# A step of a hybrid diffusion backbone: the first adaLN weights loaded in six large transfers ahead of an order of their own

## The chip, the cores and the metric

The kernel runs on one core of one Trainium2 chip. The metric is the device time of one execution in microseconds. It is written in a tile language that turns Python calls into instructions for five engines: TensorE (PE, with its weight loads shown as PEld), VectorE (DVE), ScalarE (ACT), GpSimd (POOL) and SyncE (SP), which issues all of the kernel's DMA transfers.

## What is computed

Two layers of a backbone, on 128 context tokens and 256 latent tokens together (384 columns), width 1024, all in float32. Cut to what matters here:

```python
mod = silu(c) @ w_ada[l] + b_ada[l]
shift1, scale1, gate1, shift2, scale2, gate2 = split(mod, 6)
h = rms_norm(x) * (1 + scale1) + shift1
out = mix(h)
x = x + gate1 * out
h = rms_norm(x) * (1 + scale2) + shift2
x = x + gate2 * ((silu(a_) * b_) @ w_ffn_out)
```

`mix` projects `h` with `w_in`, runs three token mixers (a state-space scan called SSD, attention, and an mLSTM), gates and merges them. So the first projection of layer 0 needs `shift1` and `scale1` of layer 0, and these need the product of a small vector with 1024 x 2048 weights (8 MB). These weights are called the first adaLN weights here.

## The kernel before

All weights lie in one array `ws` of pieces of 128 x 1024 floats (512 KB each), in the order in which they are used. `piece` (L639) loads the next piece into one of four buffers `raw` and, for a dense product, splits it on ScalarE into a high part `wh` and on VectorE (or GpSimd) into a rest `wl`, so that three fast products (`HH` with `wh`, `HL` with `wh`, `HH` with `wl`) give a float32 result; `HH` and `HL` are the two parts of the normed input. One dense piece is 8 k-tiles of three matmuls.

`setup` (L780) loads the conditioning vector (`sil`), constants (`cst`), biases (`bada`), and `x` into the slot `PH`. `ada` (L732) is called for four groups u = 0, 2, 1, 3, each with four pieces: 128 small matmuls of 32 columns with the weights `silc`, a transposition by `ident`, and an addition of the bias into `mod`. Groups 0 and 2 give shift and scale for k-tiles 0 to 3, groups 1 and 3 for 4 to 7. Meanwhile `ssq` squares x, `norm_end` (L834) makes the row factors `nacc`, and `modulate` (L858) writes `HH` and `HL`, k-tile by k-tile.

The SSD stage (`ssd`, L1002) goes over 8 pairs of heads in each layer. For a pair, `ex` (two buffers) is loaded from `rowe` by DMA and multiplied on GpSimd with `pb`; `decays` (L973) makes a decay matrix in `PH` from `PL`, which is loaded from `rowr`: VectorE writes it, ScalarE takes its exponential, GpSimd sums two halves (`PH<-PH`), VectorE multiplies it (`PH<-PH,PL`). Then TensorE adds up the pair's output in the bank `l`. Dense pieces of the projections that come later, and the attention's preparation (`E` and `D`: norms and the rotary products with `pT`), stand between the pairs.

The order of the work is not the order of the code. A recorder keeps every operation, and `order` (L376) plays a list schedule with estimated costs: whichever operation is ready and has the smallest key goes next on its engine. The key is the place in the code plus a bias set by `urgency`: FEED for loads and splits, EVAC for what empties a bank, DENSE for dense products. The costs come from `Clock` (TensorE's two rates, and a price for a change of the matmul's tile shape) and `cost`. `emit` (L503) then writes the instructions in that fixed order, at line 509, so each engine works through its own list in order; the profile shows nearly everything under L509, and tiles are told apart by name.

Of the kernel before, what the change touches and what calls it, by code (L numbers as in the profile page):

```python
# [222 lines left out]
class Recorder:  # L223
# [86 lines left out]
    class Clock:  # L310
# [9 lines left out]
        def run(self, now, work):  # L320
# [3 lines left out]
            for cols, rows, fixed, tile in work:  # L324
                if tile != self.tile:
                    now += 0.09
                    self.tile = tile
                    while now >= self.end:
                        self.tick()
                while True:  # L330
                    rate = 2400.0 if self.warm else 1200.0
                    done = min(cols, (self.end - now) * rate)
                    self.count += done * rows
                    now += done / rate
                    cols -= done
                    if cols <= 1e-6:
                        break
                    self.tick()
                if self.warm:
                    now += fixed  # L340
                while now >= self.end:
                    self.tick()
# [3 lines left out]
    def cost(eng, meth, args, kw):  # L346
# [17 lines left out]
        if eng == "sync":  # L364
            big, run = max(int(np.prod(v.shape)) for v in args[:2]), min(_run(v) for v in args[:2])
            rows = big / run
            return 0.36, rows * (0.025 + run * 4 * 0.0000415) / 16, 1.3 + min(rows, 256) * 0.0085

# [159 lines left out]
FEED, EVAC, DENSE = -60000, -30000, 60000  # L528

ND, NM, NL = 3, 4, 1  # L530
NR = 4

AHEAD = 14
# [6 lines left out]
class Net:  # L540
# [98 lines left out]
    def piece(self, key, split=True):  # L639
# [6 lines left out]
        with self.urgency(FEED):  # L646
            for _ in range(cnt):
                raw = self.buf("wp", "raw", [P, 1024], NR)
                self.dma(raw, self.I["ws"][self.ppos])
                self.ppos += 1  # L650
# [81 lines left out]
    def ada(self, l, u):  # L732
        raws = self.piece(("ada", l, u), split=False)
        ps = self.dps()
# [45 lines left out]
    def setup(self):  # L780
# [6 lines left out]
        self.cst = lambda n: cst[:, CST[n][0]:CST[n][0] + CST[n][1]]  # L787
        self.ident = self.cst("ident")
        self.badas = []
        for l in range(LAYERS):  # L790
            b = self.const(f"bada{l}", [P, 48])
            self.dma(b, I["cols"][l, :, COLS["bada"][0]:COLS["bada"][0] + 48])
            self.badas.append(b)
        self.dma(self.x, I["xT"])
        self.ones = self.const("ones", [P, P])
# [606 lines left out]
    def run(self):  # L1402
        self.setup()
        for u in (0, 2, 1, 3):
            self.ada(0, u)
        for j in range(8):
# [80 lines left out]
def layout(a):  # L1487
# [18 lines left out]
    for key, n in st:  # L1506
# [21 lines left out]
        ws[pos:pos + n] = v.reshape(P, n, 1024).transpose(1, 0, 2)  # L1528
        pos += n
    out["ws"] = ws  # L1530
    x = np.concatenate([A["x_prompt"].reshape(P, D), A["x_sample"].reshape(256, D)], axis=0)
# [63 lines left out]
```

## Time and profile before

| | us |
|---|---|
| runs | 1969.58, 1973.36, 1974.23 (median 1973.36) |
| the profiled execution's own time | 1967.48 |
| its span, first to last instruction | 1965.7 |
| TensorE busy in the span | 1904.1 (97%) |
| VectorE busy | 1295.0 (66%) |
| ScalarE busy | 951.7 (48%) |
| GpSimd busy | 371.7 (19%) |
| DMA engines, share of 16 | 53.1% for the kernel's own queue |

The profile is one execution. Busy shares are means over stages that differ: TensorE is busy nearly without a gap in most of the span, and its gaps lie in a few places. For the change the stretches at the start and the views of single engines in time order say more than the page's sums. A row of the timeline gives start, duration, engine, source line, operation, what is written and read, how many in a row, and in brackets how long the engine had been idle and on what it waited.

### The profile page before, as it was taken

To read this page: it belongs to the slowest core of one execution; us is meant where nothing else is said; L and a number is where in the kernel's file an instruction comes from. 1 tells how busy PE (TensorE), PEld (TensorE's weight loads), DVE (VectorE), ACT (ScalarE), POOL (GpSimd) and SP (SyncE) were. 2 spreads that over 40 slices of the span, in tenths; PEclk is the share of its full clock that TensorE was granted. 3 is DMA by queue.
4 is the path that set the end of the run, shared out by engine and by line. 5 is a ranking of instruction groups with operands and counts; after the bars stand their busy time and mean duration, and the time that the engine had idled before them with its cause. 6 is when DMAs were issued, how large, how long until landed. Compare 5 with 4: busy or idle time off the path is not lost. (4 is left out here: it accounts for less than half of the span.)

```text
span 1965.7 us, 30591 instructions
## 1 busy us (share of the span) xinstructions
PE 1904.1 (97%) x11202; PEld 1731.0 (88%) x11202; DVE 1295.0 (66%) x2733; ACT 951.7 (48%) x1910; POOL 371.7 (19%) x355
## 2 busy tenths in 40 slices
PE   5999999999999999999999897999999999999997
PEld 4987898789888999999999775987888999999997
DVE  4956889777745666655358677877767567666622
ACT  3654666665522444443346554666555334444421
POOL 0134433110002210001211244330000023000121
PEclk8999999999999999999999998999999999999998
DMA  8565546434488666566654655464344555444441
GB/s 298 128 173 180 151 142 193 139 107 119 128 305 273 217 193 198 188 194 193 202 184 132 163 160 124 133 184 131 116 113 145 157 169 160 118 127 129 127 124 61
DMA packets 120342, 318.33 MB, mean 162 GB/s; under 512 B 13824, under 2 KB 57216, under 8 KB 119424
## 3 DMA queue, kind: packets, MB, share of 16 engines
q1 hardware_dynamic: 120192, 316.38, 53.1%
q8 instruction: 88, 1.44, 0.3%
q14 instruction: 62, 0.51, 0.1%
HBM read 295.54 MB, written 19.74 MB: 160 GB/s over the span
## 5 line engine op out<-in xcount | busy, mean ns | idle before, releaser
L509 ACT ACTIVATE wh<-raw 128x1024 fp32r<-128x1024 f32 x374 | 396.0, 1059 | 559.9 <-PE d L509 485.1
L509 DVE TENSOR_TENSOR wl<-raw,wh 128x1024 fp32r<-128x1024 f32 x335 | 437.0, 1305 | 226.9 <-ACT wh L509 219.2
L509 PE MATMUL d<-HH,wh 128*128 128x384 f32 x1448 | 495.1, 349 | 1.6 <-ACT E L509 0.7
L509 PE MATMUL d<-HL,wh 128*128 128x384 f32 x1416 | 467.4, 336 | 0.0
L509 PE MATMUL d<-HH,wl 128*128 128x384 f32 x1384 | 465.4, 336 | 0.9 <-DVE wl L509 0.9
L509 PEld LDWEIGHTS d<-HH,wh 128*128 128x128 f32 x1448 | 272.3, 189 | 27.0 <-issue 19.2
L509 PEld LDWEIGHTS d<-HL,wh 128*128 128x128 f32 x1416 | 266.6, 189 | 1.3 <-issue 0.8
L509 PEld LDWEIGHTS d<-HH,wl 128*128 128x128 f32 x1384 | 260.5, 188 | 1.4 <-DVE wl L509 1.4
L509 PE MATMUL d<-A,wh 128*128 128x386 f32 x744 | 254.8, 342 | 0.0
L509 PE MATMUL d<-C,wh 128*128 128x386 f32 x744 | 251.5, 338 | 0.0
L509 PE MATMUL d<-A,wl 128*128 128x386 f32 x744 | 250.1, 336 | 0.0
L509 POOL TENSOR_TENSOR wl<-raw,wh 128x1024 fp32r<-128x1024 f32 x39 | 94.4, 2420 | 473.3 <-ACT sh L509 361.0
L509 PEld LDWEIGHTS d<-A,wh 128*128 128x128 f32 x744 | 139.9, 188 | 13.0 <-issue 10.9
L509 PEld LDWEIGHTS d<-C,wh 128*128 128x128 f32 x744 | 140.6, 189 | 0.4
L509 PEld LDWEIGHTS d<-A,wl 128*128 128x128 f32 x744 | 139.9, 188 | 0.0
L509 POOL TENSOR_TENSOR sc<-sc,sc 128x126 f32<-128x126 f32 x112 | 69.4, 638 | 222.8 <-DVE sc L509 203.6
L509 DVE SCALAR_TENSOR_TENSOR PH<-PL,n,cst 128x128 f32<-128x128 f32 x288 | 98.0, 375 | 16.6 <-DMA PL<-rowr 13.5
L509 DVE TENSOR_TENSOR sc<-d,nacc 128x384 f32<-128x384 f32 x93 | 51.8, 557 | 78.2 <-PE d L509 73.9
L509 PE MATMUL d<-wh,HH 128*128 128x512 f32 x240 | 98.6, 411 | 0.1
L509 PE MATMUL d<-wl,HH 128*128 128x512 f32 x240 | 94.3, 393 | 0.0
L509 PE MATMUL d<-wh,HL 128*128 128x512 f32 x240 | 94.2, 393 | 0.0
L509 PE MATMUL d<-PH,wh 128*128 128x384 f32 x256 | 87.1, 340 | 0.0
(237 smaller groups left out, 3090.6 us busy)
## 6 DMA issues: line engine op xcount, KB each, us to landing
raw<-in_ws SPq DMA_DIRECT2D x470, 512.0 KB, 3.7
PL<-rowr SPq DMA_DIRECT2D x48, 384.0 KB, 5.5
gd<-sc SPq DMA_DIRECT2D x48, 192.0 KB, 2.4
pb<-gd SPq DMA_DIRECT2D x48, 192.0 KB, 2.7
ex<-rowe SPq DMA_DIRECT2D x32, 128.0 KB, 4.0
ex<-rowe SPq DMA_DIRECT2D x16, 256.0 KB, 5.3
PH<-in_xT SPq DMA_DIRECT2D x2, 1536.0 KB, 7.3
yad<-pb SPq DMA_DIRECT2D x16, 192.0 KB, 1.9
```

The lines of the kernel that those rows point to most:

```text
L509: tc.keep_in_program_order(getattr(engines[op.eng], meth)(*[real(a) for a in args], **{k: real(v) for k, v in kw.items()}))
```

## The change

It has four parts.

- The sixteen first adaLN pieces are no longer loaded one by one into `raw`. Six transfers of 2 or 3 pieces each (FIRST_LOADS) go into slots of the later stages that are still unused: A, C, E, F, D and PL. In `ws` these pieces are laid out so that one row of such a transfer is 8 or 12 KB in one piece on both sides, instead of 4 KB.
- Setup, `x` and groups 0 and 2 get the key FIRST, groups 1 and 3 the key SECOND, and the loads of the first three dense pieces the key FIRST as well, so that these stand behind groups 0 and 2 and ahead of groups 1 and 3.
- The load of `x` moves out of `setup` to the place right behind it, ahead of all weights.
- In the planner, a change of tile shape on TensorE costs 0.18 (0.33 after the shape (4, 1), which is 128 rows by 32 columns, as in the adaLN products) instead of 0.09, and a transfer's cost per row and per byte is different. These numbers move no work by themselves; they change which operation the planner takes next, everywhere in the program.

```diff
-                    now += 0.09
+                    now += 0.33 if self.tile == (4, 1) else 0.18
...
-            return 0.36, rows * (0.025 + run * 4 * 0.0000415) / 16, 1.3 + min(rows, 256) * 0.0085
+            return 0.36, rows * (0.036 + run * 4 * 0.0000337) / 16, 1.3 + min(rows, 256) * 0.0085
...
+FIRST, SECOND = -120000, -110000
...
+FIRST_LOADS = ((0, 3, "A"), (3, 3, "C"), (6, 2, "E"), (8, 3, "F"), (11, 3, "D"), (14, 2, "PL"))
+
+AHEAD_OF_SECOND = 3
...
-                self.dma(raw, self.I["ws"][self.ppos])
+                with self.urgency(FIRST if self.ppos < 16 + AHEAD_OF_SECOND else FEED):
+                    self.dma(raw, self.I["ws"][self.ppos])
...
     def ada(self, l, u):
-        raws = self.piece(("ada", l, u), split=False)
+        key, cnt = self.stream[self.spos]
+        assert key == ("ada", l, u), key
+        self.spos += 1
+
+        for pos, n, tag in FIRST_LOADS:
+            if pos in (self.ppos, self.ppos + 3, self.ppos + 6) and self.ppos % 8 == 0:
+                home = self.slot(tag, [P, n, 1024])
+                self.dma(home.rearrange("p n c -> p (n c)"),
+                         self.I["ws"][pos:pos + n].rearrange("n p c -> (n p c)").rearrange("(p m) -> p m", p=P))
+                self.homes += [home[:, i] for i in range(n)]
+        raws = [self.homes.pop(0) for _ in range(cnt)]
+        self.ppos += cnt
...
-        self.dma(self.x, I["xT"])
...
     def run(self):
-        self.setup()
+        with self.urgency(FIRST):
+            self.setup()
+            self.dma(self.x, self.I["xT"])
         for u in (0, 2, 1, 3):
-            self.ada(0, u)
+            with self.urgency(SECOND if u % 2 else FIRST):
+                self.ada(0, u)
...
+    for at, n, _ in FIRST_LOADS:
+        ws[at:at + n] = ws[at:at + n].transpose(1, 0, 2).reshape(n, P, 1024)
```

How it moves instructions is seen in the order in which they stand on the engines. The numbers behind a name are buffers, counted anew in each program, so they differ between the two.

**SP, the start.** Before, SP's first rows are these:

```order
L509 DMA raw_80<-in_ws 128x1024
L509 DMA raw_84<-in_ws 128x1024
L509 DMA raw_86<-in_ws 128x1024
L509 DMA raw_88<-in_ws 128x1024
L509 DMA K_90<-in_ckT 128x128 x2
L509 DMA sil_2_93<-in_cT 128x16
L509 DMA cst_95<-in_cst 128x395
L509 DMA bada_4_97<-in_cols 128x48
L509 DMA bada_5_99<-in_cols 128x48
L509 DMA PH_101<-in_xT 128x3072
L509 DMA cols_103<-in_cols 128x215
```

After three rows with the conditioning vector, the constants and the first bias, SP has now:

```order
L509 DMA bada_5_88<-in_cols 128x48
L509 DMA PH_90<-in_xT 128x3072
L509 DMA A_92<-in_ws 128x3072
L509 DMA C_94<-in_ws 128x3072
L509 DMA E_96<-in_ws 128x2048
L509 DMA raw_98<-in_ws 128x1024
L509 DMA raw_102<-in_ws 128x1024
L509 DMA raw_106<-in_ws 128x1024
L509 DMA F_108<-in_ws 128x3072
L509 DMA D_110<-in_ws 128x3072
L509 DMA PL_112<-in_ws 128x2048
L509 DMA raw_114<-in_ws 128x1024
```

The four adaLN pieces that stood first are gone, x moved ahead of all weights, the three `raw` between E and F are dense pieces, and the loads of `K` and `cols` moved behind everything.

**TensorE, the end of the adaLN products.** Before, the third group (`d_259`), the broadcast of the row factors (`m_310`), the fourth group (`d_341`) and the first dense row:

```order
L509 MATMUL d_259<-raw_230,silc_82 32x128 x8
L509 MATMUL m_310<-sc_298,ones_78 128x384
L509 MATMUL d_259<-raw_245,silc_82 32x128 x8
L509 MATMUL d_338<-cst_95,sc_333 128x128
L509 MATMUL d_341<-raw_272,silc_82 32x128 x8
L509 MATMUL d_341<-raw_292,silc_82 32x128 x8
L509 MATMUL d_341<-raw_312,silc_82 32x128 x8
L509 MATMUL d_341<-raw_326,silc_82 32x128 x8
L509 MATMUL d_404<-cst_95,sc_402 128x128
L509 MATMUL d_422<-HH_329,wh_406 128x384
L509 MATMUL d_422<-HL_336,wh_406 128x384
```

Now, from the second group's transposition (`d_236`) on, with the third group `d_269`, the broadcast `m_302`, the fourth group `d_319` and the first dense piece `d_376`:

```order
L509 MATMUL d_236<-cst_84,sc_231 128x128
L509 MATMUL d_269<-F_108,silc_82 32x128 x24
L509 MATMUL m_302<-sc_280,ones_78 128x384
L509 MATMUL d_269<-D_110,silc_82 32x128 x8
L509 MATMUL d_319<-D_110,silc_82 32x128 x4
L509 MATMUL d_328<-cst_84,sc_317 128x128
L509 MATMUL d_319<-D_110,silc_82 32x128 x12
L509 MATMUL d_319<-PL_112,silc_82 32x128 x16
L509 MATMUL d_376<-HH_321,wh_224 128x384
L509 MATMUL d_376<-HL_334,wh_224 128x384
L509 MATMUL d_376<-HH_321,wl_234 128x384
L509 MATMUL d_388<-cst_84,sc_374 128x128
```

The first dense rows stand right behind the last adaLN product and ahead of its transposition (`d_388`); the broadcast still stands behind most of the third group.

**TensorE and GpSimd, SSD in layer 1.** The third, fourth and fifth pair of heads of layer 1 write the banks `l_11751`, `l_11805`, `l_11877` before. On TensorE, from the last dense row ahead of the third pair to the fourth pair's last:

```order
L509 MATMUL d_11579<-wl_11633,HH_10157 128x512
L509 MATMUL l_11751<-PH_11157,xn_11331 64x128 x2
L509 MATMUL l_11751<-ex_11318,c_1951_11326 64x256 x2
L509 MATMUL l_11751<-PH_11157,xn_11331 64x256 x4
L509 MATMUL m_11775<-cst_95,A_10466 128x128 x3
L509 MATMUL m_11783<-pb_11778,bn_10966 64x128 x2
L509 MATMUL l_11805<-PH_11157,xn_11585 64x128 x2
L509 MATMUL l_11805<-ex_11560,c_1959_11568 64x256 x2
L509 MATMUL l_11805<-PH_11157,xn_11585 64x256 x4
```

Now these three pairs are `l_11661`, `l_11785` and `l_11857`; the third pair and what follows it:

```order
L509 MATMUL l_11661<-PH_11130,xn_11310 64x128 x2
L509 MATMUL l_11661<-ex_11293,c_1941_11300 64x256 x2
L509 MATMUL l_11661<-PH_11130,xn_11310 64x256 x4
L509 MATMUL d_11583<-wh_11579,HH_10137 128x512
L509 MATMUL d_11583<-wh_11579,HL_10146 128x512
L509 MATMUL d_11583<-wl_11591,HH_10137 128x512
L509 MATMUL m_11695<-cst_84,A_10446 128x128 x3
```

Before, no dense row stood between the third and the fourth pair, nor up to the fifth, and 177 between the fifth and the sixth. Now 33 dense matmuls stand between the third and the fourth, none up to the fifth, and 36 between the fifth and the sixth. From the dense rows' total since the transpositions of the row factors, 273 stood ahead of the third pair, now 252, and ahead of the fourth and fifth 273, now 285.

On GpSimd at the same place, before (`ex_11761` is the fifth pair's, `D_11534` the attention's rotary product):

```order
L509 TENSOR_TENSOR D_11534<-D_11534,pT_5745 128x512
L509 TENSOR_TENSOR D_11534<-D_11534,pT_5853 128x8x32 x4
L509 TENSOR_TENSOR PH_11157<-PH_11157 128x384 x2
L509 TENSOR_TENSOR pb_11778<-xn_11771,we_11209 128x256
L509 TENSOR_TENSOR ex_11761<-ex_11761,pb_11033 128x512
L509 TENSOR_TENSOR PH_11157<-PH_11157 128x384 x2
L509 TENSOR_TENSOR pb_11831<-xn_11825,we_11209 128x256
L509 TENSOR_TENSOR ex_11815<-ex_11815,pb_11033 128x512
```

and now (`ex_11672` is the fifth pair's):

```order
L509 TENSOR_TENSOR PH_11130<-PH_11130 128x384 x2
L509 TENSOR_TENSOR pb_11693<-xn_11685,we_11194 128x256
L509 TENSOR_TENSOR PH_11130<-PH_11130 128x384
L509 TENSOR_TENSOR ex_11672<-ex_11672,pb_11011 128x512
L509 TENSOR_TENSOR D_11568<-D_11568,pT_5631 128x512
L509 TENSOR_TENSOR D_11568<-D_11568,pT_5771 128x8x32 x4
L509 TENSOR_TENSOR PH_11130<-PH_11130 128x384 x2
L509 TENSOR_TENSOR pb_11812<-xn_11805,we_11194 128x256
```

Before, the five rotary rows of `D` stood ahead of the third pair's second sum; now they stand behind both sums of the third pair and the fifth pair's `ex`, and ahead of the fourth pair's second sum.

## Rows read from the trace of the kernel before

**Rows 1.** Busy time of each engine in three stretches (count in brackets), clock, DMA, GB/s.

```profile
0.00:50.00 50.00, 29.65 (x314) 22.61 (x315) 21.92 (x70) 16.32 (x37) 2.64 (x12) 0.90 0.84 293
50.00:1100.00 1050.00, 1042.01 (x6094) 937.44 (x6093) 708.09 (x1466) 525.11 (x1036) 199.36 (x199) 1.00 0.57 177
1100.00:1250.00 150.00, 130.05 (x661) 105.55 (x661) 105.04 (x221) 74.37 (x139) 60.09 (x57) 0.92 0.55 148
```

**Rows 2.** Timeline of ScalarE and TensorE, 29 to 46.2 us: start, duration, work.

```profile
29.62 0.49 ACT L509 ACTIVATE nacc<-m 128x384 f32<-128x384 f32 x1 [4.58 <-PE m L509]
...
36.80 1.08 PE L509 MATMUL d<-raw,silc 128*32 128x128 f32 x16 [2.31 <-DMA raw<-in_ws]
...
39.28 0.69 PE L509 MATMUL d<-HH,wh 128*128 128x384 f32 x1 [0.47 <-ACT wh L509]
...
41.19 0.69 PE L509 MATMUL d<-HH,wl 128*128 128x384 f32 x1 [0.90 <-DVE wl L509]
...
45.52 0.49 PE L509 MATMUL d<-HH,wh 128*128 128x384 f32 x1
...
45.84 0.35 PE L509 MATMUL d<-HL,wh 128*128 128x384 f32 x1
...
46.02 0.33 PE L509 MATMUL d<-HH,wl 128*128 128x384 f32 x1
```

**Rows 3.** Stretches of the transfers, columns as in rows 1.

```profile
3.50:13.00 9.50, 2.95 (x56) 2.73 (x60) 0.35 (x2) 0.21 (x1) 0.00 (x0) 1.00 1.02 388
...
14.50:19.50 5.00, 1.84 (x21) 1.28 (x20) 3.73 (x11) 2.93 (x8) 0.00 (x0) 1.00 1.01 404
...
32.00:38.00 6.00, 2.42 (x52) 1.34 (x48) 3.58 (x11) 2.07 (x5) 0.00 (x0) 0.80 0.96 362
...
39.28:45.84 6.56, 5.66 (x17) 5.16 (x18) 6.56 (x13) 4.16 (x8) 0.00 (x0) 0.50 0.67 200
...
671.00:676.00 5.00, 5.00 (x31) 5.00 (x30) 2.52 (x3) 1.36 (x2) 0.00 (x0) 1.00 0.92 362
```

**Rows 4.** Timeline of TensorE in layer 1, 1184 to 1203 us.

```profile
1184.98 0.39 PE L509 MATMUL d<-wh,HL 128*128 128x512 f32 x1
...
1185.20 0.39 PE L509 MATMUL d<-wl,HH 128*128 128x512 f32 x1
...
1192.85 0.48 PE L509 MATMUL l<-PH,xn 128*64 128x128 f32 x1 [6.89 <-DVE PH L509]
...
1202.48 0.47 PE L509 MATMUL l<-PH,xn 128*64 128x128 f32 x1 [4.46 <-DVE PH L509]
```

**Rows 5.** Timeline of GpSimd in layer 1, 1178 to 1200 us.

```profile
1178.70 2.21 POOL L509 TENSOR_TENSOR D<-D,pT 128x512 f32<-128x512 f32 x1 [1.90 <-DVE D L509]
...
1181.54 4.22 POOL L509 TENSOR_TENSOR D<-D,pT 128x256 f32<-128x256 f32 x4 [0.63 <-DVE D L509]
...
1199.12 1.45 POOL L509 TENSOR_TENSOR ex<-ex,pb 128x512 f32<-128x512 f32 x1 [1.80 <-DMA ex<-rowe]
```

**Rows 6.** Chain of waits in time order: start, us, what; 1194 to 1202 us.

```profile
1194.92 4.04 DMA ex<-rowe
...
1200.54 1.04 POOL PH L509
```

**Rows 7.** Timeline of SP, first 8 us: start, duration, line, transfer, count.

```profile
0.73 1.81 SPq L509 DMA_DIRECT2D raw<-in_ws  x4
...
3.85 0.44 SPq L509 DMA_DIRECT2D sil<-in_cT  x1
...
4.34 0.47 SPq L509 DMA_DIRECT2D cst<-in_cst  x1
...
4.85 1.19 SPq L509 DMA_DIRECT2D bada<-in_cols  x2
...
7.26 0.33 SPq L509 DMA_DIRECT2D PH<-in_xT  x1
```

**Rows 8.** Tile raw, first 60 us, its last line.

```profile
DMA to landing us min/median/max: 3.5/4.8/6.7
```

More of the change, by code (lines that the diff above doesn't have):

```diff
@@ L788, in setup @@
         self.ident = self.cst("ident")
+        self.homes = []
         self.badas = []
```

## The prediction, on record before the changed kernel was run

> **What bounds the kernel now.** I read first the busy time of the engines in long stretches [rows 1]. TensorE is busy for 1042.0 of the 1050 us between 50 and 1100: there it is the bound, and no earlier transfer helps. Two stretches differ. In the first 50 us it is busy for 29.65, so 20.35 us are idle, and between 1100 and 1250 us for 130.05 of 150, so 19.95 are idle. The change works on the first by its code and on the second by the planner's new prices.
>
> Then the timeline at the start. TensorE's dense work begins at 39.28 us, but only from 41.19 does it run on: its first row of the low part waited 0.90 for `wl` [rows 2]. Ahead of that it worked on the last adaLN piece at 36.80, for which it had waited 2.31 on the DMA [rows 2]. So transfers set the beginning, and behind them a short chain: product, transposition, split of the first dense piece. The transfers run at 388 to 404 GB/s where the queue is full, at 362 just before the last piece lands [rows 3].
>
> Last, layer 1's SSD stage. TensorE waits 6.89 us before the third pair and 4.46 before the fourth, both for VectorE's `PH` [rows 4]; the chain of waits shows why the fourth takes 9.63 us after the third (1202.48 less 1192.85): a load of `ex` of 4.04 us, GpSimd's multiplication, then GpSimd's sum of `PH`, which stands behind it in GpSimd's list [rows 4 to 6].
>
> **Term 1, the beginning.** SP now starts with `sil`, `cst` and two `bada`: 0.44 + 0.47 + 1.19 = 2.1 us [rows 7], and gaps. So `x` is issued near 3.0, where before the first large load went out at 0.73. A 512 KB load lands 3.5 us after its issue at the shortest [rows 8]; take off SP's 0.33 and 1.3 for 524 KB at 395 GB/s, and 1.9 us are left for its start and its end together. I take 1.0 for each, so the stream runs from 4.0. From there to the last adaLN piece it carries `x`, A, C, F and D of 1536 KB, E and PL of 1024 KB and three dense `raw` of 512 KB: 11264 KB = 11.53 MB. None of these waits for a buffer, where before SP waited for a free `raw` after every four pieces.
>
> The rate is not known for six large loads in a row. Rows: 404 GB/s with 512 KB loads, 388 with x among them, 362 in 32 to 38 us, and 362 around the second load of x, whose rows are 12 KB like the new ones [rows 3]. Nothing there is faster for long rows, so I take 395, between the first two because their queue was full as the new one will be. That is 29.2 us; the last byte moves at 33.2, and with the 1.0 for its end PL has landed at 34.2. The Trainium skill has a limit against this: DMA: Bandwidth & Descriptors, section Where 436 GB/s comes from, puts what HBM gives one core at about 358 GB/s and says that it binds for loads; by it the burst would take 32.2 us. The trace disagrees with its 404 over 5 us, though its 362 would fit.
>
> Then 16 small matmuls at 1.08 us [rows 2] bring 35.3. The first dense rows stand right behind, their weights split long before, so the old 2.5 us from the last product's start to the first dense row and the 0.90 for `wl` fall away; the transposition among them costs about 0.5. Is the normed input ready? The broadcast of the row factors stands behind most of the third group, which needs F: 8.91 MB, landed near 27.6. Its 24 small matmuls (1.6), itself (1.0) and ScalarE's copy of 0.49 end at 30.7, against 30.1 before [rows 2]; then ScalarE must first copy the third group's result, which needs D at 31.5, and the first k-tile is there near 33.5. That is before 35.3, and TensorE's list runs two further dense pieces on the early k-tiles while VectorE writes the later ones. `cols`, now behind PL, lands near 36 and can hold VectorE for under 1 us; `K`, `c` and the rotary table are wanted much later.
>
> The clock: at 39.28 to 45.84 the granted clock is 0.50, 1.2 GHz, and matmuls follow each other every 0.32 us; at 45.84 the next comes after 0.18, at 2.4 GHz [rows 2, 3]. TensorE had waited before. It will have waited now, too, so I let as many run at the low level: 17 of them from 35.8 on, 5.4 us, to 41.2, where before 17 were done at 45.84 [rows 3]. **Gain 4.6.** Ends: at 404 GB/s, where the burst takes 28.5, 5.3; at 362, where it takes 31.9, 1.9; and below nothing a loss of 5.6 at 293, the mean of the first 50 us with all waits for buffers in it [rows 1], which I take for a far end only.
>
> **Term 2, layer 1's SSD stage.** Work there is the same, the order is not. Before TensorE reaches the third pair it has now 21 dense matmuls fewer behind it, at 0.22 [rows 4] 4.6 us: near 1180.9 instead of 1185.5. VectorE's and GpSimd's part of that pair no longer stands behind the attention's products of `D` (2.21 + 4.22 us on GpSimd) [rows 5], which is what made it late, so I let this wait go. What is late next is the fourth pair: its second sum now stands behind the fifth pair's `ex` and behind the products of `D`. From the third pair's start: 2.07 until the load (1194.92 less 1192.85), 4.04 for it, the multiplication with its start 6.27 after and 1.45 long, 6.43 for the products, and 1.9 from the sum to the matmul (1202.48 less 1200.54) [rows 4 to 6]: 16.1, or 17 with an estimated 0.9 for VectorE's sum of the products. So the fourth pair starts near 1198, 4.5 earlier than at 1202.48, and TensorE has done 12 more dense matmuls by then, 2.6 us. The link to the fifth pair stays. Between the fifth and the sixth there are only 36 dense matmuls, 6.5 us at 0.18, against a link of 9.63: 3.1 lost. **Gain 4.5 + 2.6 - 3.1 = 4.0.** Ends: a whole link, 9.6, if the third pair comes earlier still; nothing below, for the third pair may stay late, which is a rival.
>
> **Other edits.** Elsewhere the new prices move some 5% of TensorE's rows. Where it is busy nearly throughout, a swap of ready work costs nothing; I put 0, with 2 either way for layer 0's SSD stage, whose pairs keep at least 39 dense matmuls between them. The new layout in `ws` is made before the run.
>
> **Sum.** 4.6 + 4.0 = 8.6. Against the profiled execution's own 1967.48 that is 1958.9. This execution is 5.9 below the median of the runs, 1973.36; set against that median, **1964.8 us**.
>
> **Rivals.** *Only the beginning gains.* If the waits of layer 1 merely change places, 4.6 is left: 1968.8. For it: two links are unfilled before and after. *The burst runs at 362 GB/s*, as just before the last piece: term 1 is 1.9, the time with term 2 is 1967.5. For it: that is also the rate around the second x load [rows 3]; against: the 404. By the limit of the Trainium skill named above it would be nearly the same. *The dense weights do not help:* they delay the last adaLN piece by 1.57 MB, 4.0 us, and if the row factors come late (F and D later than reckoned), TensorE waits for `HH` instead; term 1 is then 0 and the time 1969.4. *Slower:* the rotary products of `D`, now behind the fifth pair's `ex` on GpSimd, hold the fourth pair. If the third pair comes as late as before, at 1192.85, the fourth comes 17 later, near 1209.9, 7.4 after its old time, and with 3.1 before the sixth pair 10.5 are lost, if VectorE holds the dense pieces' splits back as well; less 4.6, that is 1979.3. It decides from the third pair's start: with these 3.1, later than about 1187 the stage eats the whole of term 1.
>
> **How the numbers follow.** Both terms as reckoned 0.50, its own range 1957 to 1970; only the beginning 0.15; slow burst 0.15; dense weights no help 0.06; slower 0.14. About 0.3%, 5.9 us, is what a measurement can tell from no change. Faster by more: 0.45 of the first, 0.04 + 0.06 + 0.01 of the next three: 0.56. Slower by more: 0.09 of the last, 0.01 + 0.02 from others: 0.12. Between: 0.32. The range 1955 to 1976 leaves out most of the slower case and gains over 18 us, some 0.16.
>
> **What would show it.** Right: PL lands at 33 to 36, dense rows run on from about 36, at 2.4 GHz from about 41 to 42; the third pair without a wait, the fourth some 17 us behind it; under 17 us idle between 1100 and 1250. Wrong: a first dense row that waits for `HH`; transfers well below 388 GB/s from 5 to 33 us; more idle in layer 1; or new gaps between 50 and 1100.

## The result: slower, and not where the change works

The changed kernel took **1986.68 us** (median of 4 runs, 1985.74 to 1986.97), the kernel before 1973.37 (4 runs, 1969.58 to 1974.23): a ratio of 1.007 (95% interval 1.0053 to 1.0088), 13 us slower, where 8.6 us less had been forecast. A second measurement on another chip gave 1.0079 (1.0066 to 1.0092). The profiled execution of the change took 1986.97 us, its span is 1985.2, 19.5 more than before.

TensorE's busy time on the page of the changed kernel:

```profile
span 1985.2 us, 30537 instructions
...
PE 1927.5 (97%) x11202; PEld 1745.8 (88%) x11202; DVE 1292.5 (65%) x2733; ACT 950.8 (48%) x1910; POOL 364.3 (18%) x355
```

Before, the same 11202 matmuls were busy for 1904.1 us. So on the whole TensorE doesn't wait longer; it is busy 23.4 us longer with the same work. Busy times in the stretches of [rows 1], changed kernel (columns: stretch, its length, PE, PEld, DVE, ACT, POOL busy with counts, granted clock, share of the DMA engines, GB/s):

```profile
0.00:50.00 50.00, 29.13 (x347) 24.27 (x348) 23.40 (x72) 18.75 (x40) 2.84 (x12) 0.90 0.76 293
50.00:1100.00 1050.00, 1044.96 (x6010) 934.34 (x6011) 694.88 (x1449) 514.30 (x1023) 191.99 (x195) 1.00 0.58 176
1100.00:1250.00 150.00, 130.74 (x653) 101.73 (x652) 105.68 (x219) 73.89 (x137) 57.85 (x56) 0.91 0.53 146
```

The first 50 us went about as forecast: 347 matmuls instead of 314, so 33 more, which is 5.8 us at 0.176. Then between 50 and 1100 us TensorE is busy 2.95 us longer and does 84 matmuls fewer. There most of the loss arises, in the stretch to which the prediction gave 0: layer 1's SSD stage, whose first matmul is shown below, begins 12.6 us later than before.

What makes TensorE slower can be seen in two pieces of the chain of waits in which nothing but dense matmuls stands (start, us, what, count). The first is 912 matmuls of 384 columns from `HH`, `HL`, `PH` and `PL`; the second 1512, two thirds of 386 columns from `A` and `C`. The kernel before:

```profile
1512.73 158.14 PE d L509 x912
1678.21 264.42 PE d L509 x1512
```

The changed kernel:

```profile
1526.32 160.89 PE d L509 x912
1694.74 267.62 PE d L509 x1512
```

Per matmul that is 173.4 ns before and 176.4 now (158.14 and 160.89 by 912), and 174.9 and 177.0 in the second. The first piece begins 13.6 us later than before, the span ends 19.5 later, and the 5.9 between are these two pieces, 2.75 and 3.20 longer. TensorE waits for nothing there, the clock is granted at 1.00, the weights and operands are the same numbers. Only two things differ: the order of instructions, and the place of the tiles in SBUF (the on-chip memory from which TensorE reads). With `PH`, `A`, `C`, `E`, `F`, `D` and `PL` wanted first, as homes for `x` and the adaLN weights, they are also allocated first. In the built programs `HH` begins at byte 80800 of each partition before and at 154112 now, counted modulo 256 at 160 and at 0. The same for others: `HL` 160 and 0, `D` 160 and 0, `PL` 224 and 0, `F` 64 and 0, `A` 160 and 224, `C` 64 and 32; `PH` 224 in both. All weights (`wh`, `wl`) begin at 160 in both.

The beginning itself, timeline of TensorE in the changed kernel (start, duration, work):

```profile
34.77 1.06 PE L509 MATMUL d<-PL,silc 128*32 128x128 f32 x32
35.76 0.44 PE L509 MATMUL d<-HH,wh 128*128 128x384 f32 x1
36.04 0.34 PE L509 MATMUL d<-HL,wh 128*128 128x384 f32 x1
36.22 0.33 PE L509 MATMUL d<-HH,wl 128*128 128x384 f32 x1
```

The first dense row stands at 35.76 (35.3 had been forecast; 39.28 before [rows 2]) and has not waited; the next come after 0.28 and 0.18, so at 2.4 GHz from the second on, where 17 at 0.32 had been put in.

Layer 0's SSD stage has a wait that was not there before. TensorE and GpSimd in the changed kernel, timeline:

```profile
168.48 0.44 PE L509 MATMUL m<-pb,bn 128*64 128x128 f32 x4 [3.01 <-POOL pb L509]
```

```profile
165.60 1.27 POOL L509 TENSOR_TENSOR ex<-ex,pb 128x512 f32<-128x512 f32 x1 [4.88 <-DMA ex<-rowe]
166.82 1.60 POOL L509 TENSOR_TENSOR pb<-xn,we 128x256 f32<-128x256 f32 x1
```

The product `pb`, for which TensorE waits, stands on GpSimd behind a product of `ex` that waits 4.88 us for a load. And behind TensorE's wait of 3.01 us the granted clock falls to 1.2 GHz, stretches of the changed kernel:

```profile
160.00:169.50 9.50, 6.49 (x40) 5.93 (x39) 8.09 (x21) 5.36 (x12) 3.54 (x3) 1.00 0.54 157
169.50:180.00 10.50, 10.50 (x30) 7.82 (x30) 3.84 (x14) 3.29 (x6) 2.28 (x2) 0.51 0.60 129
180.00:190.00 10.00, 10.00 (x56) 7.36 (x55) 2.87 (x4) 3.36 (x8) 7.44 (x7) 1.00 0.41 116
```

So in this execution a wait of 3.0 us costs another 5: 10.5 us are busy throughout at half the clock, with 30 matmuls where the next 10 us have 56.

Layer 1's SSD stage, timeline of TensorE: first the stage's first matmul in the kernel before,

```profile
1126.81 0.36 PE L509 MATMUL m<-cst,pb 64*128 64x64 f32 x1 [4.92 <-ACT pb L509]
```

then the changed kernel, from the same matmul to the second half of the fourth pair, the place of the waits in [rows 4]:

```profile
1139.37 0.36 PE L509 MATMUL m<-cst,pb 64*128 64x64 f32 x1 [7.67 <-ACT pb L509]
...
1191.73 0.44 PE L509 MATMUL l<-PH,xn 128*64 128x128 f32 x4
...
1202.19 0.43 PE L509 MATMUL l<-PH,xn 128*64 128x128 f32 x2
...
1212.37 0.48 PE L509 MATMUL l<-PH,xn 128*64 128x128 f32 x1 [9.74 <-DVE PH L509]
```

and GpSimd beside it:

```profile
1196.49 1.43 POOL L509 TENSOR_TENSOR ex<-ex,pb 128x512 f32<-128x512 f32 x1 [0.59 <-DMA ex<-rowe]
1198.90 7.32 POOL L509 TENSOR_TENSOR D<-D,pT 128x512 f32<-128x512 f32 x5 [0.98 <-DVE D L509]
1210.30 1.15 POOL L509 TENSOR_TENSOR PH<-PH 128x384 f32<-128x384 f32 x1 [4.08 <-ACT PH L509]
```

The third pair (1191.73) no longer waits, as forecast. The fourth waits 9.74 in its second half, 20.6 us behind the third pair's start. Idle time between 1100 and 1250 is 19.3 us, against 19.95, but this window holds other work now, for the stage begins later.

### The profile page after: what moved, and what is told of

Read it like the earlier page. It is cut to its first block, busy times and chain, and to the rows that moved or that the text cites. A ratio compares the mean times of both kernels' runs of the same rounds, so it can differ in the third digit from the quotient of the medians.

```text
span 1985.2 us, 30537 instructions
## 1 busy us (share of the span) xinstructions
PE 1927.5 (97%) x11202; PEld 1745.8 (88%) x11202; DVE 1292.5 (65%) x2733; ACT 950.8 (48%) x1910; POOL 364.3 (18%) x355
## 5 line engine op out<-in xcount | busy, mean ns | idle before, releaser
L509 ACT ACTIVATE wh<-raw 128x1024 fp32r<-128x1024 f32 x374 | 396.0, 1059 | 580.1 <-PE d L509 506.4
L509 DVE TENSOR_TENSOR wl<-raw,wh 128x1024 fp32r<-128x1024 f32 x335 | 432.1, 1290 | 257.6 <-ACT wh L509 254.0
L509 PE MATMUL d<-HH,wh 128*128 128x384 f32 x1448 | 499.4, 352 | 0.2 <-ACT sc L509 0.2
L509 PE MATMUL d<-HL,wh 128*128 128x384 f32 x1416 | 472.8, 339 | 0.0
L509 PE MATMUL d<-HH,wl 128*128 128x384 f32 x1384 | 469.3, 339 | 0.0
L509 PEld LDWEIGHTS d<-HH,wh 128*128 128x128 f32 x1448 | 272.1, 189 | 24.4 <-issue 20.2
L509 PEld LDWEIGHTS d<-HL,wh 128*128 128x128 f32 x1416 | 266.4, 189 | 2.0 <-issue 0.8
L509 PEld LDWEIGHTS d<-HH,wl 128*128 128x128 f32 x1384 | 260.6, 188 | 0.0
L509 PE MATMUL d<-A,wh 128*128 128x386 f32 x744 | 255.6, 344 | 0.0
L509 PE MATMUL d<-A,wl 128*128 128x386 f32 x744 | 252.5, 339 | 0.0
L509 PE MATMUL d<-C,wh 128*128 128x386 f32 x744 | 251.9, 339 | 0.0
L509 POOL TENSOR_TENSOR wl<-raw,wh 128x1024 fp32r<-128x1024 f32 x39 | 93.5, 2397 | 462.7 <-ACT sh L509 365.2
L509 PEld LDWEIGHTS d<-A,wh 128*128 128x128 f32 x744 | 140.0, 188 | 13.0 <-issue 12.6
L509 PEld LDWEIGHTS d<-C,wh 128*128 128x128 f32 x744 | 140.7, 189 | 0.4
L509 PEld LDWEIGHTS d<-A,wl 128*128 128x128 f32 x744 | 140.3, 189 | 0.0
L509 DVE SCALAR_TENSOR_TENSOR PH<-PL,n,cst 128x128 f32<-128x128 f32 x288 | 99.4, 382 | 20.4 <-DMA PL<-rowr 15.4
L509 DVE TENSOR_TENSOR sc<-d,nacc 128x384 f32<-128x384 f32 x93 | 51.8, 557 | 82.6 <-PE d L509 78.0
L509 POOL TENSOR_TENSOR sc<-sc,sc 128x126 f32<-128x126 f32 x112 | 65.7, 606 | 194.0 <-DVE sc L509 148.8
L509 PE MATMUL d<-wh,HH 128*128 128x512 f32 x240 | 100.8, 420 | 0.0
L509 PE MATMUL d<-wh,HL 128*128 128x512 f32 x240 | 95.7, 399 | 0.0
L509 PE MATMUL d<-wl,HH 128*128 128x512 f32 x240 | 95.4, 398 | 0.0
L509 PE MATMUL d<-PH,wh 128*128 128x384 f32 x256 | 87.4, 341 | 0.0
```

Of the source, the lines that this page charges most:

```text
L509: tc.keep_in_program_order(getattr(engines[op.eng], meth)(*[real(a) for a in args], **{k: real(v) for k, v in kw.items()}))
```

## The experiments

The theory from here on: **address.** The distance of dense matmuls (from one start to the next) depends on where their two operands begin in SBUF, and the new order of allocation moved them to a worse place. The rival: **order.** The distance comes from the new order of instructions, which the planner's prices made, or from `wh` and `wl`, two of whose buffers changed places. A further question is what the new prices cost by their waits. All ratios are to the kernel before, run on the same chip beside the experiment, with a 95% interval.

**e1, the change with 160 unused bytes ahead of its slots** (order unchanged, `HH` at 160 modulo 256 again):

```
             net.run()
+            net.pools["sp"].tile([P, 40], F32, tag="pad", name="pad")
             net.rec.emit(tc)
```

> The changed kernel with 160 unused bytes ahead of the slots in SBUF, so that HH, HL, D, F and PL begin where they began before the change, counted modulo 256 (160 instead of 0 for HH); the order of all instructions is that of the change. Theory address (the 8736 dense matmuls follow each other more slowly because their operands moved in SBUF): the steady distance of dense matmuls falls from 176.7 back to about 173.4 ns, TensorE's busy time by some 20 us, the time to 1963 to 1970 us. Rival order (the distance comes from the new order of instructions or from wh and wl having changed places in SBUF): distance 176 to 177 ns and a time of 1983 to 1990 us, as without the bytes.

Measured: 1972.92 us, ratio 1.0027 (1.0017 to 1.0036). The chain's two pieces:

```profile
1512.17 158.77 PE d L509 x912
1678.47 266.47 PE d L509 x1512
```

The first is at 174.1 ns a matmul, nearly as before; the second at 176.2, not yet, for the bytes put `A` at 128 and `C` at 192, where neither had been. Not one instruction has changed its place in any list. The rival, order, falls for the 384 columns. The forecast of 1963 to 1970, made against 1973.37 us for the kernel before, is a ratio of 0.9947 to 0.9983; it was missed by 0.0044, some 9 us, in part since it supposed the same gain for 386 columns: by the starts in the traces 5 us of the dense matmuls' loss are left. It also says that `F` and `PL` are back at their old places; before they began at 64 and 224, here at 160.

**e2, the kernel before with 96 unused bytes**, the same line with 24 elements:

> The kernel before with 96 unused bytes ahead of the slots, so that HH and HL begin at 0 modulo 256, as they do in the changed kernel; nothing else differs. Theory address: dense distance up from 173.4 to 176 or 177 ns, TensorE busy some 20 us longer, time 1990 to 1998 us. Rival order: 173.4 ns and 1970 to 1976 us.

Measured: 1977.20 us, ratio 1.0051 (1.0036 to 1.0066): slower, by half of what was expected.

```profile
1518.08 159.83 PE d L509 x912
1685.24 265.98 PE d L509 x1512
```

With `HH` and `HL` at 0 the kernel before becomes slow without any change to its work. It is only half, and the reason is in part argued: the other slots were moved too, and `PH` and `PL`, a good part of the first piece, now begin at 64, which e4 shows to be a fast place. By the starts in the traces the dense matmuls that follow one another took 13 us more than before in e2, against 17.4 in the changed kernel, so the 20 expected were too many in any case.

**e3, the change with the planner's old prices:**

```
-                    now += 0.33 if self.tile == (4, 1) else 0.18
+                    now += 0.09
...
-            return 0.36, rows * (0.036 + run * 4 * 0.0000337) / 16, 1.3 + min(rows, 256) * 0.0085
+            return 0.36, rows * (0.025 + run * 4 * 0.0000415) / 16, 1.3 + min(rows, 256) * 0.0085
```

> The changed kernel with the planner's two old prices (0.09 for a change of the tile's form, the old price of a transfer); the new beginning stays. HH stays at 0 modulo 256. Theory address: the dense distance stays at 176.7 ns; what the new prices cost goes: the wait of 3.01 us for pb in layer 0's SSD stage, the 10 us at half clock behind it (5 us) and some of layer 1's, so 1978 to 1983 us. Rival order by prices: the dense distance is the new order's doing and falls to 173.4 ns, time 1963 to 1970 us.

Measured: 1978.97 us, ratio 1.0058 (1.0041 to 1.0075); by ratio the forecast was 1.0023 to 1.0049, so this is slower than expected. The chain has `1687.00 267.62 PE d L509 x1512`, to the hundredth what the change has, in another order. The wait for `pb` at 168 us is gone and the clock is granted at 1.00 there. Prices do not make the distance; they do make that wait.

**e4, a table of addresses.** The kernel before, with 64 groups of 32 matmuls of 384 columns behind the output, operand and weights each at 0, 32, ... 224 modulo 256:

```
+            for i in range(8):
+                for j in range(8):
...
+                    a, b = (32 * i - 160) % 256 // 4, (32 * j - 160) % 256 // 4
+                    for k in range(32):
+                        w = b + 128 * (k % 8)
+                        self.mm(o[:, 0:NTOK], st[:, w:w + 128], mv[:, a:a + NTOK], k == 0, k == 31)
```

> The kernel before with 2048 more matmuls of 384 columns behind the output, in 64 groups of 32: the moving operand begins at 0, 32, ... 224 modulo 256 (first letter a to h of the name of the group's bank), the weights too (second letter). Theory address: the groups differ; qff (160 and 160, the kernel before) takes about 173.3 ns for each matmul, qaf (0 and 160, the changed kernel) 176 or more. Rival order: all 64 groups take 173 to 174 ns. The time itself is about 370 us longer than before and says nothing.

Timeline of TensorE behind the output; the first letter after q is the operand's start, the second the weights' (a is 0, b 32, ... h 224):

```profile
1997.76 5.81 PE L509 MATMUL qaf<-HH,HL 128*128 128x384 f32 x32
2003.40 5.71 PE L509 MATMUL qag<-HH,HL 128*128 128x384 f32 x32
...
2221.53 5.73 PE L509 MATMUL qff<-HH,HL 128*128 128x384 f32 x32
2227.09 5.71 PE L509 MATMUL qfg<-HH,HL 128*128 128x384 f32 x32
...
2311.04 5.71 PE L509 MATMUL qhf<-HH,HL 128*128 128x384 f32 x32
2316.60 5.81 PE L509 MATMUL qhg<-HH,HL 128*128 128x384 f32 x32
```

From one start to the next: `qaf`, the changed kernel's `HH`, 5.64 us by 32 = 176.3 ns; `qff`, the same tile before, 5.56 = 173.8; `qhf`, `PH` in both, 5.56. A step of 0.01 us in a start is 0.3 ns here. The whole table, worked out in this way, depends on one number, the weights' start less the operand's, modulo 256, but for two groups that fall out, `qga` and `qba` (six groups in the first row, for the first of all ran at the low clock and the last has no next; eight in the others):

| weights less operand | ns a matmul, lowest to highest group |
|---|---|
| 0 | 173.8 to 174.1 |
| 32 | 173.4 to 174.1 |
| 64 | 174.7 to 175.0, one group 176.6 |
| 96 | 173.1 to 173.4 |
| 128 | 175.9 to 176.3 |
| 160 | 176.3 to 176.6 |
| 192 | 173.4 to 173.8 |
| 224 | 176.6, one group 173.1 |

Before, `HH`, `HL` and `D` had 0 and `PH` and `PL` 192; in the changed kernel `HH`, `HL`, `D`, `F` and `PL` have 160, one of the two slowest. This is the address theory measured by itself. It is a difference of two addresses, so neither is "aligned" or not alone.

It is not the whole rule for the kernel, where matmuls with different operands take turns. By the starts in the traces, a matmul on `PH` with one on `PL` behind it took 173.4 ns before, 175.9 in the changed kernel and 174.2 in e6 (below), though `PH` and the weights kept their places modulo 256 in all three and only `PL` moved. How a neighbour's address enters was not measured.

**e5, the change again,** unaltered:

> The changed kernel itself, unaltered, beside the others on the same chip. Its ratio to the kernel before was 1.007 (1.0053 to 1.0088); it should come again. If the half clock at 170 us of the first profile is chance, it may be gone here, and the ratio 0.002 to 0.003 lower.

Measured: 1984.49 us, ratio 1.0079 (1.0066 to 1.0092); 160.88 us for the 912 matmuls. Half clock came again, though for a shorter time: it is no chance of one run.

**e6, the change with all slots at good places,** 32 to 192 unused bytes ahead of five of them:

```
+PADS = {"A": 192, "C": 96, "E": 96, "HH": 32, "B": 32}
...
         if self.real is None:
+            if self.tag in PADS and (self.pool, self.tag) not in PADDED:
+                PADDED.append((self.pool, self.tag))
+                self.pool.tile([P, PADS[self.tag] // 4], F32, tag=f"pad_{self.tag}", name=f"pad_{self.tag}")
             self.real = self.pool.tile(list(self.shape), self.dtype, tag=f"{self.tag}_{self.place}", name=self.name)
```

> The changed kernel with unused bytes ahead of five slots (192 A, 96 C, 96 E, 32 HH, 32 B), so that A, C, E, HH, HL and F2 begin where they began before the change, modulo 256, and D, F, PL and B at 128 or 64, for which the table of the fourth experiment has 173.3 ns. The order of instructions is the change's. Theory address alone: 384 columns 173.9, 386 columns 175.6 and 512 columns 228.4 ns apart, as before the change; 14 + 4 + 4 = 22 us less than the change, so a ratio to the kernel before of 0.995 to 0.999: what is left is the beginning's gain of 6 or 7 us less what the new order costs in the two SSD stages. Rival, the new order costs more than the beginning brings: the same distances, but a ratio of 1.001 or more.

Measured: 1967.99 us, ratio 0.9995 (0.9986 to 1.0004), against 1.0079 of e5: the places are worth 0.0084, 16.5 us.

```profile
1512.51 158.35 PE d L516 x912
1678.40 264.79 PE d L516 x1512
```

Both pieces are back at the old distance. Busy in the stretch from 300 to 1100 us, first before the change, then changed, then here:

```profile
300.00:1100.00 800.00, 799.13 (x4731) 717.99 (x4729) 516.57 (x1080) 379.30 (x788) 112.47 (x97) 1.00 0.58 184
```

```profile
300.00:1100.00 800.00, 799.13 (x4672) 714.13 (x4671) 506.07 (x1063) 370.02 (x775) 110.33 (x93) 1.00 0.58 183
```

```profile
300.00:1100.00 800.00, 799.13 (x4708) 713.83 (x4707) 512.56 (x1074) 376.65 (x785) 110.02 (x94) 1.00 0.58 183
```

The busy time is the same to the hundredth in all three: in a stretch where TensorE is always busy only the counts show the loss. Here 36 of the 59 lost matmuls are back; the other 23 may be another mix of work, for the order is still the change's. But the ratio lies between the two forecasts, 0.999 and 1.001: what the beginning brings, something else still takes.

**e7, the same with the old prices** (the diff of e3):

> The same with the planner's old prices. If the new order of the SSD stages costs what the beginning brings (3 us by the wait for pb near 166 us, 2 to 3 us in layer 1), this one is 3 to 6 us faster than the aligned change, a ratio of 0.994 to 0.997. If the prices do nothing on balance, the two are equal within 0.2%.

Measured: 1961.24 us, ratio 0.9955 (0.9942 to 0.9969). So the two new prices cost 0.0040, 8 us, and the beginning alone brings 9.

**e8, tables for 386 and 512 columns.** As e4; 64 groups of 42 matmuls in the pattern of `A` and `C` (386 columns, rows of 1544 bytes, weights at 160), then 8 groups of 32 with 512 columns, operand at 160.

> The kernel before with two more tables behind the output. First 64 groups of 42 matmuls in the pattern of the stage with A and C: 386 columns, rows of 1544 bytes, weights at 160; the first letter is where A begins modulo 256 in steps of 32, the second where C begins. Theory address: the groups differ by some 5 ns; qfc (160 and 64, the kernel before) near 175.6, qhh (224 and 224, the changed kernel) near 177.4. Then 8 groups of 32 with 512 columns, where the weights begin at 0 to 224 and the moving operand at 160: sf (before) near 227, sa (the change) near 234. Rival: no differences. The time says nothing.

The letters there have a slip: `C` lies at 32 in the changed kernel, so `qhb` is its group. The 512 columns, timeline:

```profile
2454.78 7.60 PE L509 MATMUL sb<-D,HH 128*128 128x512 f32 x32
...
2484.47 7.42 PE L509 MATMUL sf<-D,HH 128*128 128x512 f32 x32
2491.73 7.62 PE L509 MATMUL sg<-D,HH 128*128 128x512 f32 x32
```

`sf`, as before the change, takes 7.26 us by 32 = 226.9 ns; `sa`, the changed kernel, 234.1 from its first start at 2447.29. In the first table `qfc` (before) takes 175.2 ns (7.36 us from its first start to the next group's, by 42), `qhb` (changed) 177.4, and the lowest of all, `qfa`, 174.8. So 384, 386 and 512 columns each have their own fast differences: at 96, fast with 384, 512 columns are slow.

**e9 to e11, the prices one by one.** e9 is the kernel before with both new prices (its slots stay); e10 and e11 are e7 with one new price each, e10 that of a change of form, e11 that of a transfer.

> The kernel before with the planner's two new prices alone; its slots stay where they were. Theory: the prices cost by themselves what the seventh run got back against the sixth, so a ratio to the kernel before of 1.002 to 1.005, with a wait for pb of about 3 us and half clock in layer 0's SSD stage, near 172 us. Rival, they harm only behind the new beginning: 0.999 to 1.001.

> The aligned change, the new price for a change of the tile's form, the old price for a transfer. If this price makes the wait for pb in layer 0 and its half clock, the ratio to the kernel before is near that of the sixth run, 0.998 to 1.000; if not, near the seventh's, 0.995 to 0.997.

> The aligned change, the old price for a change of form, the new price for a transfer. The counterpart of the run above: 0.995 to 0.997 if the price of a change of form does the harm, 0.998 to 1.000 if the price of a transfer does.

Measured: e9 1976.35 us, 1.0034 (1.0020 to 1.0047); e10 1958.60 us, 0.9941 (0.9927 to 0.9955); e11 1959.08 us, 0.9945 (0.9932 to 0.9957). e10 and e11 came out below both ranges that they had been given: behind the new beginning neither price alone does harm, the two together do. With the old beginning the two together cost as well (e9); one by one they were not tried there. e9 has the wait for `pb`, 2.49 us at 172.69, and the half clock behind it; e10 and e11 have neither. In e9 two buffers of `wh` and `wl` have changed places as in the changed kernel, and its two dense pieces take 158.32 and 264.43 us, as before: so neither this exchange nor an order by the new prices makes the matmuls slow. e10 and e11 beat both kernels of this case.

**e12, e7 without dense weights in the middle:**

```
-AHEAD_OF_SECOND = 3
+AHEAD_OF_SECOND = 0
```

> The seventh run's kernel (aligned, old prices) with no dense weights in the middle of the first loads: all six adaLN loads first, then the dense ones. If the weights in the middle are worth what the prediction's first term gave them, the first dense matmul comes 2 to 3 us later than 38 us and the ratio to the kernel before is 0.996 to 0.998, against 0.9955. Rival, their transfer is hidden and PL's earlier landing makes up for it: 0.995 to 0.996.

Measured: 1967.05 us, ratio 0.9984 (0.9972 to 0.9997). The first dense rows wait for their splits, timeline of TensorE:

```profile
36.07 0.45 PE L516 MATMUL d<-HH,wh 128*128 128x384 f32 x1 [0.61 <-ACT wh L516]
37.84 0.69 PE L516 MATMUL d<-HH,wl 128*128 128x384 f32 x1 [1.15 <-DVE wl L516]
```

The first dense matmul came at 36.07, not 2 to 3 us behind e7's 37.78, but those behind it stood further apart. The dense weights in the middle are worth 0.0029, some 6 us, more than expected; by the traces e12 is 2.8 us behind e7 at the start of the 501st dense matmul, and the rest has no one place.

**e13, one exchange on GpSimd.** e6 (both new prices) with `pb` ahead of the `ex` that waits for its load, in layer 0 alone:

```
...
+        for a, b in zip(gp, gp[1:]):
+            if out(a) == "ex" and out(b) == "pb" and "we" in src(b) and self.ops[a].start < 400:
+                plan.remove(a)
+                plan.insert(plan.index(b) + 1, a)
```

> The sixth run's kernel (aligned, both new prices) with two instructions of GpSimd exchanged in layer 0's SSD stage: the multiplication of pb now stands ahead of the multiplication of ex that waits for its load, and no longer behind it. Theory queue: xn is ready at 163 us, so pb is done before TensorE wants it at 165.5; the wait of 3.16 us and the half clock behind it go, 4 to 5 us, and the ratio to the kernel before falls from 0.9995 to 0.997 to 0.998. Rival: ex is then late by what pb takes, and the wait moves to the pair of ex: 0.999 to 1.000.

Measured: 1962.42 us, ratio 0.9977 (0.9962 to 0.9992). Timeline of GpSimd and TensorE in e6:

```profile
163.59 1.26 POOL L516 TENSOR_TENSOR ex<-ex,pb 128x512 f32<-128x512 f32 x1 [5.08 <-DMA ex<-rowe]
164.81 1.60 POOL L516 TENSOR_TENSOR pb<-xn,we 128x256 f32<-128x256 f32 x1
...
166.46 0.44 PE L516 MATMUL m<-pb,bn 128*64 128x128 f32 x4 [3.16 <-POOL pb L516]
```

and in e13:

```profile
161.65 0.62 POOL L524 TENSOR_TENSOR pb<-xn,we 128x256 f32<-128x256 f32 x1 [2.41 <-ACT xn L524]
...
163.82 0.44 PE L524 MATMUL m<-pb,bn 128*64 128x128 f32 x4
...
164.02 1.29 POOL L524 TENSOR_TENSOR ex<-ex,pb 128x512 f32<-128x512 f32 x1 [1.76 <-DMA ex<-rowe]
```

The stretch behind it (columns as above), e6 and then e13:

```profile
168.00:178.00 10.00, 10.00 (x31) 7.67 (x32) 3.72 (x11) 3.69 (x6) 2.28 (x2) 0.51 0.55 138
```

```profile
168.00:178.00 10.00, 10.00 (x58) 7.39 (x57) 7.70 (x14) 5.47 (x12) 7.51 (x7) 1.00 0.78 222
```

Wait and half clock are both gone, 58 matmuls instead of 31 stand in the same 10 us, and `ex` comes late for nobody. By the ratios the exchange gives 0.0018, 3.5 us, with intervals that overlap; by the spans of the two profiled executions, 1965.9 and 1959.8, it gives 6.1. The theory of the queue stands by the trace, where the wait went and came nowhere else in this stretch; its size does not stand as firmly.

**e14, e11 with `C` at 0,** the best place of e8's table (`PADS` with 32 for `C`, 160 for `E`):

> The eleventh run's kernel (aligned, old price for a change of form, new price for a transfer) with C moved from 64 to 0 modulo 256, for which the eighth run has 174.7 ns with 386 columns against 175.4. Theory address: 2190 matmuls by 0.7 to 0.9 ns are 1.5 to 2 us, a ratio to the kernel before of 0.9935 to 0.994 against 0.9945. Rival, the table does not carry over from 7 to 8 k-tiles: 175.6 ns and 0.9945.

Measured: 1959.60 us, ratio 0.9964 (0.9949 to 0.9979), and 265.64 us for the 1512 matmuls, where e11 has 264.79. A miss: the better place in the table is not the better one here. The table was made with 7 k-tiles and one pair of starts at a time, and the stage has 8; whether that is the reason was not tested. With 386 columns the rows begin 1544 bytes apart, so each k-tile has another difference. The old places stay the best that was measured in the stage itself.

## Why the prediction was wrong

**What bounds the kernel:** right. TensorE is the bound between 50 and 1100 us, and so every nanosecond on a dense matmul is lost time. This was said, and its other side was not seen: the argument watched what TensorE waits for, never how fast it works.

**Term 1, the beginning, gain 4.6:** right in mechanism, under-sized by the clock. A stretch of the changed kernel:

```profile
8.00:16.00 8.00, 2.86 (x49) 2.50 (x49) 3.35 (x6) 3.41 (x8) 0.00 (x0) 1.00 1.00 427
```

`PL` landed at 34.1 (issued at 13.02, landed 21.1 later), where 34.2 had been forecast, but that is luck: two errors cancel. The burst ran at 427 GB/s, and at 410 on the mean of 4 to 34.2 us, where 395 had been taken, between 388 and 404 [rows 3]. In that time it moved 12.4 MB, not 11.53, for SP issued the next `raw` at 16.71 and other loads soon after, ahead of `PL`'s landing. By the Trainium skill (DMA: Bandwidth & Descriptors, Where 436 GB/s comes from) some 358 GB/s should have bound; the trace disagrees, with 427 over 8 us. The same section also names a measurement of 425, which fits.

The part that was mis-sized is the 17 matmuls at the low clock, 5.4 us, which were not there: TensorE had worked on the adaLN products up to the first dense row, and the clock, granted at 0.50 from 24 to 32 us, was at 0.91 on the mean from 32 to 38. At 0.18 the 17 take 3.1, so 2.4 us more were gained, an estimate of 7.0 in all. The 33 more matmuls by 50 us are 5.8 us; at the start of the 501st dense matmul the changed kernel is 6.0 us ahead of the kernel before (133.71 and 139.67), and e7 7.1. By its ratio e7, in which little else is changed, gives 9 us.

**Term 2, layer 1, gain 4.0:** the waits moved in part as said, and nothing was gained. The whole stage begins 12.6 us later, at 1139.37, so times are counted from its first matmul. TensorE stood at the third pair after 52.4 us and did not wait, as said; before, it was there after 58.7 (the prediction's 1185.5) and waited until 66.0 [rows 4]. So the third pair came early enough for a gain, by the prediction's own measure. The fourth pair's second half came 20.6 us behind the third's start, not 17, and waited 9.74 of them: the rival's mechanism, `D`'s products ahead of the pair's sum, 7.32 us here where 6.43 had been put in. It still came after 73.0 us, against 75.7 before. From the stage's first matmul to the 912 dense ones the kernel before takes 385.9 us and the changed one 387.0, with slower matmuls; in e6, where they are back at the old distance, it is 384.3 (1128.17 to 1512.51), a gain of 1.6. Against this the wait for `pb` just ahead grew from 4.92 to 7.67, in e6 to 7.05, which no term had. So there was no gain of 4.0 and no loss of 10.5. No run has this stage's new order alone.

**Other edits, 0 with 2 either way: the step that failed.** It was put as "a swap of ready work costs nothing". Two things were missed, and together they cost more than both terms could bring.

- The places of the slots. They were no term at all. The change takes its homes from slots "still free", and the first use decides where a slot lies. e1, e2 and e4 show the cause, and e6 against e5 the size, 16.5 us. The traces agree: by the starts, 1 to 3 ns more on most of some 8000 dense matmuls with 384 and 386 columns and 6 on 720 with 512 add up to 17.4 us in the changed kernel, and to nothing in e6 (0.4 less than before).
- The two new prices. Together they cost 8 us against the old ones (e6 and e7), 10 against either alone (e10, e11), 7 with the old beginning (e9). Some 3.5 of it, by ratios whose intervals overlap, is one pair of instructions on GpSimd in layer 0 (e13): a wait of 3 us, and the low clock behind it, which cost 5 more in the profiled execution of the change and less in e5's, and which the prediction had priced only at the start. What lies between e13 at 0.9977 and e10 and e11 at 0.9941 and 0.9945 stays open.

The steps from the kernel before to the change: the beginning and either price, 0.9943 (e10, e11); the second price, 0.0052 (e6); the places, 0.0084 (e5), which ends at e5's 1.0079. They add up because each is the difference of two neighbours, so the sum is no check of its own. Of the rivals, the one that ended slower named a mechanism that took place, but not the one that decided. Of the four things named as signs of being wrong, one came, a new gap between 50 and 1100 (the 3.01 us for `pb`), but none was the one that decided: not a wait and not a gap, but a busy time that grew.

## What to carry to other kernels

When a change lets tiles be touched in another order, compare the addresses that they get, before and after, and count matmuls in a stretch in which TensorE never waits: a fully busy engine can still do fewer of them. Where a kernel is bound by dense matmuls, measure the distance for a few starts of operand and weights, and in the stage itself too, since a table need not carry over (e14); then pin the good ones with a few unused bytes. Here 448 bytes gave back 16.5 us. And a wait of some 3 us on TensorE in a busy stage has to be priced with the low clock that may follow it, so look on the other engines for short products that stand behind one that waits for a load.

## What the hardware showed that was not expected

- **The distance of matmuls depends on two addresses.** With 384 columns 173.1 to 176.6 ns were measured, by the weights' start less the operand's modulo 256 bytes (e4), and 226.9 to 234.1 with 512 (e8). The Trainium skill (TensorE: Matmul & The Clock Gate, Wait — 56ns, not 53.3ns?) has, for back-to-back matmuls, the columns by 2.4 GHz, which is 160.0 and 213.3 ns here, and a fixed 2.5 ns beyond them; in this kernel, whose operands are 4 bytes wide and whose every matmul has its own weight load, it is 13 to 21 and not fixed. Why the difference matters inside the chip is not shown by any run here.
- **One wait, two costs.** Waits of 3.01, 3.16 and 3.33 us for `pb` in layer 0 (change, e6, e5) were followed by 10.2, 10.2 and 3.4 us at 1.2 GHz; 2.55 us (e1) by none, but 2.49 (e9) by 10.2. So the length of the wait alone does not tell what follows.
- **Loads ran at 427 GB/s** from 8 to 16 us with rows of 12 KB, above the 404 seen with rows of 4 KB [rows 3]. That the long rows make the difference is not shown: from 16 to 24 us, in which the three `raw` with rows of 4 KB were loaded for the greater part, it was 424.
